# Attention scores on four quarters of the TensorE array (64 queries by 192 keys) in place of two row halves (128 queries by 256 keys)

## The chip, the cores and the metric

The program runs on one core of a Trainium2 chip. The metric is device time in microseconds of one execution; lower is better.

## What is computed

A two-layer decoder trunk over 1024 tokens of width 1024, in fp32. Layer 0 mixes retention and RWKV-7 heads, layer 1 is sliding-window attention with a learned sink per head; each layer ends with a SwiGLU feed-forward block. The change is in the attention:

```python
# SWA_WINDOW = W = 128, 16 query heads, 4 key/value heads, head size 64
kb, vb = with_prev(k), with_prev(v)          # own block of 128 keys and the one before
s = jnp.einsum('bnqhgd,bnkhd->bnhgqk', q, kb).astype(jnp.float32) * HEAD_DIM ** -0.5
rel = qi + W - kj
band = (rel >= 0) & (rel < W)
valid = band[None] & ((jnp.arange(NB)[:, None, None] > 0) | (kj[None] >= W))
s = jnp.where(valid[None, :, None, None], s, -jnp.inf)
m = jnp.maximum(jnp.max(s, axis=-1, keepdims=True), sink)
e = jnp.exp(s - m)
p = e / (jnp.sum(e, axis=-1, keepdims=True) + jnp.exp(sink - m))
o = jnp.einsum('bnhgqk,bnkhd->bnqhgd', p.astype(vb.dtype), vb)
```

So each query sees exactly 128 keys: query t of a block sees its own block's keys 0..t and the earlier block's keys t+1..127.

## The kernel before, in words

Activations lie with features on partitions and tokens along the free dimension. The projections and feed-forward products are done as three fp32r matmuls per 128x512 tile (high and low parts, lines 1298, 1300, 1301 and 445 to 448); attention's own matmuls are plain fp32, and the trace shows each of those as two MATMUL records, each with a weight load. TensorE (PE) runs nearly all the time.

Attention (`attn`, line 1679) is called for the two halves of 512 tokens, hf = 0 and hf = 1. Each call works through 16 blocks, one per key/value head g and 128-query block b (g outer). A block holds 4 query heads; they lie in pairs i on the two partition halves e, and the keys of a head are kept on both halves (tiles kc and ks). Block j goes through three stages, shifted against each other, in a generator loop (line 1761): `turn(j-2)`, `out(j-3)`, `scores(j)`.

- `scores(j)` (line 1693): for each i and each e one matmul of 128 queries against 256 keys (contraction 64, so the two e are on the two row halves of the array) into the PSUM tile of e, tags "r" and "c", one buffer each (lines 1702 to 1709). Then the band is folded to 128 columns: ACT copies the earlier block's half to s (line 1715), and DVE overwrites with the own block's half where the key is not later than the query (COPY_PREDICATED, line 1716). The first 128 tokens (hf = 0, b = 0: blocks 0, 4, 8 and 12, called first blocks below, `k0 = 1`) have no earlier block: there the matmuls take 128 keys, and DVE adds a mask of 0 and -1e30 (line 1713), without ACT. Then row maximum (1719), sink (1721, 1722), four exponentials on ACT (1725), sum and reciprocal (1726, 1727), and the scaling of s, half on POOL and half on DVE (1729).
- `turn(j)` (line 1734): four PE transposes of s (1739), and DVE multiplies the result by the two triangle masks (1741).
- `out(j)` (line 1743): probabilities times values on the two column halves of the array (1751), evacuated by ACT (1757) and DVE (1758).

The fill between the stages are projections and feed-forward tiles of the same layer. The order of PE's instructions in this part is written out by hand, the table ATTN_ORDER (line 135): `39,40:4` takes 4 matmuls in turn from PSUM tiles number 39 and 40 (`queue`, line 326). The orders of DVE, ACT and POOL come from the scheduler of the language.

```python
blocks = [(g, b) for g in range(4) for b in range(4)]
...
for j in range(n + 3):
    if 0 <= j - 2 < n:
        turn(j - 2)
    if 0 <= j - 3 < n:
        n8 = n8 or outs()
        out(j - 3)
    if j < n:
        scores(j)
```

Of the kernel before, what the change touches and what calls it, by code (L numbers as in the profile page):

```python
# [52 lines left out]
def make_consts():  # L53
    c = np.zeros((P, NCO), np.float32)

    def put(name, v):
        o, w = CO[name]
        c[: v.shape[0], o : o + w] = v.reshape(v.shape[0], w)
# [36 lines left out]
        g2[64:, p] = gm[2 * p + 1]  # L95
    put("gam", g2)
    own = np.tri(P, dtype=np.float32)
    put("amask", np.concatenate([own, np.where(own > 0, 0.0, -1e30), own.T, 1.0 - own.T], axis=1))
    put("eps", np.tile(np.array([[RMS_EPS, RET_EPS, RWKV_EPS, math.log(0.5)]], np.float32), (P, 1)))
    return c  # L100

# [31 lines left out]


ATTN_ORDER = """
# [13 lines left out]
"""  # L149


# [102 lines left out]
class Kern:  # L254
# [32 lines left out]
    def mm(self, out, lhsT, rhs, **kw):  # L287

        i = self.nc.tensor.matmul(out, lhsT, rhs, **kw)  # L289
        self.order(out, i)  # L290
        n = 1
        for v in rhs.shape[1:]:
            n *= v
        if rhs.dtype == F32R:
            self.plan.now += 0.000443 * n
        else:
            self.plan.now += max(0.05, 0.00167 * n * (0.6 if lhsT.shape[0] <= 64 or lhsT.shape[1] <= 64 else 1.0))
# [1312 lines left out]
    def attn_open(self, ap):  # L1610
        nc = self.nc
        m = self.const(ap, "amask").rearrange("p (m o t) -> p m o t", m=4, o=1)
        self.own, self.add = (m[:, i].to_broadcast([P, 2, P]) for i in range(2))
        self.sides = [m[:, i].to_broadcast([P, 4, P]) for i in (3, 2)]
        self.sink = self.t(ap, [P, 16], "sink")
        nc.scalar.dma_start(self.sink, self.A["sinks"].to_broadcast([P, 16]))
        self.nsink = self.t(ap, [P, 16], "nsink")
        nc.vector.tensor_scalar(out=self.nsink, in0=self.sink, scalar1=-1.0, scalar2=None, op0=ALU.mult)
        self.b8 = self.t(ap, [P, 8], "b8")
        nc.vector.tensor_scalar(  # L1620
            out=self.b8, in0=self.pv[:, PV["bqkv"] : PV["bqkv"] + 8], scalar1=0.125, scalar2=None, op0=ALU.mult
        )
        self.pk = self.pvt = None
        self.akv, self.aq, self.ch = {}, ([], []), {}
# [54 lines left out]
    def attn(self, hf, ap, outs, fill):  # L1679
# [13 lines left out]
        def scores(j):  # L1693
# [2 lines left out]
            g, b = blocks[j]  # L1696
            ti, rg = g // 2, g % 2
            k0 = first(b)
            kw = slice(P * k0, 256)
            s = sm[j] = self.t(ap, [P, 4, P], "s", 3)  # L1700
            pss = [self.pst("rc"[e], [P, 2, 256]) for e in range(2)]
            for i in range(2):
                for e in (1, 0):
                    a = slice(64 * e, 64 * e + 64)
                    src = (kc if e == rg else ks)[ti]
                    mm(
                        pss[e][:, i, kw], qt[2 * g + i][a, P * b : P * b + P], src[a, P * b + P * k0 : P * b + 256],
                        start=True, stop=True,
                    )
            for e in range(2):  # L1710
                o = s.rearrange("p (i e) k -> p e i k", e=2)[:, e]
                if k0:
                    V.tensor_tensor(out=o, in0=pss[e][:, :, P:], in1=self.add, op=ALU.add)
                else:
                    S.copy(o, pss[e][:, :, :P])
                    V.copy_predicated(o, self.own.bitcast(mybir.dt.uint32), pss[e][:, :, P:])
            st4 = self.t(ap, [P, 4, 4], "st4", 4)
            m, den, es = st4[:, 0, :], st4[:, 1, :], st4[:, 2, :]
            V.tensor_reduce(out=m, in_=s, axis=AX.X, op=ALU.max, negate=True)
# [325 lines left out]
```

## Time and profile before

| | |
|---|---|
| median of 3 runs | 2278.35 us (2278.09 to 2280.45) |
| the profiled execution's own time | 2278.55 us |
| its span | 2276.8 us |
| PE busy | 2247.2 us, 99% of the span |
| DVE, ACT, POOL busy | 1677.0, 1023.6, 999.3 us |
| granted TensorE clock | 0.998 of full speed over the span |
| attention's part of the span | about 1362 to 1646 us |

The span is what the trace covers; the execution's own time is 1.75 us longer. A matmul's end is modelled in this trace and overlaps its successor, so how long PE takes for a group is read from the start of one instruction to the start of the next.

### The profile page before, as it was taken

The numbers are of one execution on the slowest core, as the hardware profiler recorded it, in microseconds if no ns is written. First come the engines' busy times: TensorE is split into PE (matmuls) and PEld (weight loads), VectorE is DVE, ScalarE is ACT, GpSimd is POOL, SyncE is SP. The second block draws the span as 40 slices with busy tenths as digits, with TensorE's granted clock in tenths as the row PEclk, the third lists the DMA queues.
The fourth block names the chain that finished last, engine by engine and source line by source line (L and its number), as shares of the span: only waits on it lengthen the run. The fifth ranks groups of instructions, "written<-read, shape, count | busy, mean of one in ns | idle before, by whom it ended". The sixth has DMA issues, their size and how long they took to land.

```text
span 2276.8 us, 35457 instructions
## 1 busy us (share of the span) xinstructions
PE 2247.2 (99%) x12944; PEld 1796.9 (79%) x12944; DVE 1677.0 (74%) x2600; ACT 1023.6 (45%) x1943; POOL 999.3 (44%) x796
## 2 busy tenths in 40 slices
PE   8999999999999999999999999999999999999998
PEld 6777777778878888888888887687788888888886
DVE  7877965876667358888885967857657788888866
ACT  5454544434455333333343466547654333333335
POOL 3123221212341067777777600103103677777675
PEclk9999999999999999999999999999999999999999
DMA  8565644444356455655767342123246466557663
GB/s 282 187 215 196 206 157 135 141 125 128 134 185 217 168 179 206 215 208 208 261 221 260 113 125 72 53 93 126 100 141 226 172 214 215 209 199 287 228 220 116
DMA packets 170333, 406.53 MB, mean 179 GB/s; under 512 B 43184, under 2 KB 45744, under 8 KB 170160
## 3 DMA queue, kind: packets, MB, share of 16 engines
q1 hardware_dynamic: 166752, 397.59, 50.7%
q10 hardware_dynamic: 2832, 4.59, 0.6%
q8 instruction: 103, 1.69, 0.3%
q0 software_dynamic: 576, 2.10, 0.2%
q14 instruction: 70, 0.57, 0.1%
HBM read 275.61 MB, written 123.21 MB: 175 GB/s over the span
## 4 chain that ended last, share of the span: by engine, by line
PE 80%; DVE 8%; ACT 3%; DMA 3%; issue 3%; POOL 1%; SPq 1%; DVEq 0%; POOLq 0%; ACTq 0%
PE ps_f L289 10%; PE ps_m L1298 7%; PE ps_m L1301 7%; PE ps_m L1300 7%; PE ps_f L1298 6%; PE ps_m L289 6%; PE ps_f L1300 6%; PE ps_f L1301 6%; PE ps_f L448 2%; PE ps_f L445 2%; PE ps_f L447 2%; PE ps_r L1301 2%; PE ps_r L1298 2%; PE ps_c L1301 2%; PE ps_r L1300 2%
## 5 line engine op out<-in xcount | busy, mean ns | idle before, releaser
L289 PE MATMUL ps_f<-n,w 128*128 128x512 f32 x1440 | 359.7, 404 | 8.5 <-ACT w L430 5.8
L289 PEld LDWEIGHTS ps_f<-n,w 128*128 128x128 f32 x1440 | 268.4, 190 | 82.5 <-issue 12.6
L431 POOL TENSOR_TENSOR w<-wr,w 128x512 fp32r<-128x512 f32 x63 | 86.7, 1383 | 301.1 <-ACT w L430 299.3
L430 ACT CAST w<-wr 128x512 fp32r<-128x512 f32 x231 | 141.2, 618 | 165.6 <-PE ps_f L448 58.6
L431 DVE TENSOR_TENSOR w<-wr,w 128x512 fp32r<-128x512 f32 x168 | 120.7, 721 | 61.3 <-ACT w L430 60.7
L1298 PE MATMUL ps_f<-n,w 128*128 128x512 f32 x415 | 164.4, 396 | 0.0
L1300 PE MATMUL ps_f<-n,w 128*128 128x512 f32 x415 | 162.8, 392 | 0.0
L1301 PE MATMUL ps_f<-n,w 128*128 128x512 f32 x415 | 162.6, 392 | 0.0
L431 POOL TENSOR_TENSOR w<-wq,w 128x512 fp32r<-128x512 f32 x91 | 130.4, 1444 | 32.7 <-ACT w L430 32.7
L1298 PE MATMUL ps_m<-n,w 128*128 128x512 f32 x333 | 130.6, 392 | 0.2 <-DMA n<-hc 0.2
L1300 PE MATMUL ps_m<-n,w 128*128 128x512 f32 x333 | 129.6, 389 | 0.0
L1301 PE MATMUL ps_m<-n,w 128*128 128x512 f32 x333 | 129.6, 390 | 0.0
L1308 DVE TENSOR_TENSOR nq<-ps_m,u 128x512 f32<-128x512 f32 x88 | 58.9, 684 | 93.6 <-PE ps_m L1301 93.5
L1729 POOL TENSOR_TENSOR s<-s,st 128x256 f32<-128x256 f32 x32 | 22.9, 715 | 186.4 <-DVE st L1727 76.5
L462 POOL TENSOR_TENSOR n<-nq,n 128x512 fp32r<-128x512 f32 x60 | 100.0, 1678 | 7.7 <-ACT n L460 7.6
L1493 POOL TENSOR_TENSOR w<-wd,w 128x512 fp32r<-128x512 f32 (+1 forms) x62 | 86.7, 1408 | 33.9 <-ACT w L1492 31.6
L1298 PEld LDWEIGHTS ps_f<-n,w 128*128 128x128 f32 x415 | 77.9, 188 | 20.8 <-issue 3.4
L1298 PE MATMUL ps_m<-cb,w 128*128 128x512 f32 x236 | 91.9, 389 | 0.3 <-DVE nq L1308 0.3
L1300 PEld LDWEIGHTS ps_f<-n,w 128*128 128x128 f32 x415 | 77.9, 188 | 18.0 <-issue 2.3
L1301 PE MATMUL ps_m<-cb,w 128*128 128x512 f32 x236 | 91.8, 389 | 0.0
L1300 PE MATMUL ps_m<-cb,w 128*128 128x512 f32 x236 | 91.8, 389 | 0.0
L1301 PEld LDWEIGHTS ps_f<-n,w 128*128 128x128 f32 x415 | 77.9, 188 | 16.8 <-issue 0.7
(523 smaller groups left out, 6421.2 us busy)
## 6 DMA issues: line engine op xcount, KB each, us to landing
hc<-n SPq DMA_DIRECT2D x84, 512.0 KB, 3.4
wsp<-w SPq DMA_DIRECT2D x54, 512.0 KB, 3.5
w<-wsp SPq DMA_DIRECT2D x54, 512.0 KB, 3.4
n<-hc SPq DMA_DIRECT2D x54, 512.0 KB, 6.4
wq<-in_w_gate SPq DMA_DIRECT2D x44, 512.0 KB, 4.5
u<-u SPq DMA_DIRECT2D x88, 256.0 KB, 3.0
ha<-hc SPq DMA_DIRECT2D x34, 512.0 KB, 5.3
hid<-n SPq DMA_DIRECT2D x66, 256.0 KB, 2.0
```

Of the source, the lines that this page charges most:

```text
L289: i = self.nc.tensor.matmul(out, lhsT, rhs, **kw)
L430: nc.scalar.copy(hi[:, :n], raw[:, c])
L431: self.lo.tensor_tensor(out=lo[:, :n], in0=raw[:, c], in1=hi.bitcast(F32)[:, :n], op=ALU.subtract)
L445: x = nc.tensor.matmul(ps, hi, rh, start=k == 0, stop=False)
L447: y = nc.tensor.matmul(ps, hi, rl, start=False, stop=False)
L448: z = nc.tensor.matmul(ps, lo, rh, start=False, stop=k == n - 1)
L462: e.tensor_tensor(out=lo, in0=src, in1=hi.bitcast(F32), op=ALU.subtract)
L1298: i = mm(ps, hi, xh, start=first and k == 0, stop=False, skip_group_check=True)
L1300: mm(ps, hi, xl, start=False, stop=False, skip_group_check=True)
L1301: mm(ps, lo, xh, start=False, stop=last and k == len(w) - 1, skip_group_check=True)
L1308: self.last_add = V.tensor_tensor(out=o, in0=x, in1=y, op=ALU.add)
L1493: nc.gpsimd.tensor_tensor(out=lo, in0=v, in1=hi.bitcast(F32), op=ALU.subtract)
```

## The change

The scores of a block are formed by 64 queries (x = 0 and x = 1, the two column halves of the array) in place of 128. Query half 0 needs 192 keys, the earlier block and the first half of its own; query half 1 needs the second half of the earlier block and all of its own. Both are laid into 192 PSUM columns: the columns 0 to 127 hold what is never masked on the diagonal, the columns 128 to 191 the 64 keys on the diagonal. Query half 0 is one matmul of 192 keys, query half 1 one of 128 keys, whose output goes to two runs of 64 columns (0 and 128), and one of 64 keys. The predicated copy now takes the diagonal 64 columns against a mask that is nonzero only in the two diagonal squares. First blocks take four parts (128 and 64, 128 and 64), and get the predicated copies as well as the mask addition.

```diff
+    x = np.arange(P) // 64
+    diag = np.where(x[:, None] == x[None, :], own, 0.0)
+    put("amask", np.concatenate([diag, np.where(x[:, None] > x[None, :], 0.0, -1e30), own.T, 1.0 - own.T], axis=1))
...
 ATTN_ORDER = """
-22:24 27:1 23:4 24:2 26,25:4 27:18 28:4 29:4 30,31:4 27:5 36:16 32:4 33:4 35:1 34:2 35:1 37:4 38:4 39,40:4 36:8 41:24
+20,21:12 22:24 27:1 23:4 24:2 25,26:12 27:18 28:4 29:4 30,31:16 27:5 36:16 32:4 33:4 34,35:12 37:4 38:4 39,40:12 36:8
...
+        self.diag = m[:, 0].rearrange("p o (x t) -> p o x t", x=2).to_broadcast([P, 2, 2, 64])
+        self.add = m[:, 1].to_broadcast([P, 2, P])
...
-            pss = [self.pst("rc"[e], [P, 2, 256]) for e in range(2)]
+            pss = [self.pst("rc"[e], [P, 2, 192]) for e in range(2)]
+            k1 = P * b + P
+            kp = k1 - P * (1 - k0)
             for i in range(2):
-                for e in (1, 0):
-                    a = slice(64 * e, 64 * e + 64)
-                    src = (kc if e == rg else ks)[ti]
-                    mm(
-                        pss[e][:, i, kw], qt[2 * g + i][a, P * b : P * b + P], src[a, P * b + P * k0 : P * b + 256],
-                        start=True, stop=True,
-                    )
+                parts = [(0, slice(kp, kp + 192), slice(0, 192))]
+                if k0:
+                    parts = [(0, slice(k1, k1 + P), slice(0, P)), (0, slice(k1, k1 + 64), slice(P, 192))]
+                parts.insert(1, (1, slice(k1, k1 + P), None))
+                parts.append((1, slice(kp + 64, kp + P), slice(64, P)))
+                for x, kk, c in parts:
+                    for e in (1, 0):
+                        a = slice(64 * e, 64 * e + 64)
+                        o = pss[e][64 * x : 64 * x + 64, i]
+                        o = o[:, c] if c else o.rearrange("p (y t) -> p y t", t=64)[:, 0:3:2]
+                        r = (kc if e == rg else ks)[ti][a, kk]
+                        mm(
+                            o, qt[2 * g + i][a, P * b + 64 * x : P * b + 64 * x + 64],
+                            r if c else r.rearrange("p (y t) -> p y t", t=64), start=True, stop=True,
+                            skip_group_check=True,
+                        )
             for e in range(2):
                 o = s.rearrange("p (i e) k -> p e i k", e=2)[:, e]
                 if k0:
-                    V.tensor_tensor(out=o, in0=pss[e][:, :, P:], in1=self.add, op=ALU.add)
+                    V.tensor_tensor(out=o, in0=pss[e][:, :, :P], in1=self.add, op=ALU.add)
                 else:
                     S.copy(o, pss[e][:, :, :P])
-                    V.copy_predicated(o, self.own.bitcast(mybir.dt.uint32), pss[e][:, :, P:])
+                V.copy_predicated(
+                    o.rearrange("p i (x t) -> p i x t", x=2), self.diag.bitcast(mybir.dt.uint32),
+                    pss[e][:, :, P:].rearrange("p i (o t) -> p i o t", o=1).to_broadcast([P, 2, 2, 64]),
+                )
```

On PE nothing moves except inside the score groups. Block 3's group before (queries, tile q, against keys, tiles kc and ks; the last number is the free size) and now:

```order
L1751 MATMUL ps_y_12985<-pT_12903,vt_12393 64x256 x2
L1706 MATMUL ps_r_12991<-kc_1902_12394,q_1926_12556 128x256
L1706 MATMUL ps_c_12992<-ks_1907_12430,q_1926_12556 128x256
L1706 MATMUL ps_r_12991<-kc_1902_12394,q_1926_12556 128x256
L1706 MATMUL ps_c_12992<-ks_1907_12430,q_1926_12556 128x256
```

```order
L1768 MATMUL ps_y_13015<-pT_12925,vt_12393 64x256 x2
L1719 MATMUL ps_c_13022<-ks_1907_12430,q_1926_12556 64x192
L1719 MATMUL ps_r_13021<-kc_1902_12394,q_1926_12556 64x192
L1719 MATMUL ps_c_13022<-ks_1907_12430,q_1926_12556 64x2x64
L1719 MATMUL ps_r_13021<-kc_1902_12394,q_1926_12556 64x2x64
L1719 MATMUL ps_c_13022<-ks_1907_12430,q_1926_12556 64x64
L1719 MATMUL ps_r_13021<-kc_1902_12394,q_1926_12556 64x64
L1719 MATMUL ps_c_13022<-ks_1907_12430,q_1926_12556 64x192
L1719 MATMUL ps_r_13021<-kc_1902_12394,q_1926_12556 64x192
```

Four matmuls became twelve (the last four are not shown), sixteen in a first block.

On DVE two instructions are added to each first block, between the mask addition and the row maximum. Block 4 before (s is the block's score tile, st its statistics) and now:

```order
L1758 TENSOR_TENSOR n_1999_12981<-ps_y_13045,n_1995_12977 128x2x128
L1713 TENSOR_TENSOR s_13052<-ps_c_13054,c_amask_12331 128x2x128
L1713 TENSOR_TENSOR s_13052<-ps_r_13053,c_amask_12331 128x2x128
L1634 TENSOR_TENSOR kc_2009_13015<-ps_f_13024,rs_12721 128x512
L1719 TENSOR_REDUCE st_2020_13061<-s_13052 128x4
```

```order
L1775 TENSOR_TENSOR n_1999_13011<-ps_y_13083,n_1995_13007 128x2x128
L1727 TENSOR_TENSOR s_13090<-ps_c_13092,c_amask_12331 128x2x128
L1727 TENSOR_TENSOR s_13090<-ps_r_13091,c_amask_12331 128x2x128
L1730 COPY_PREDICATED s_13090<-c_amask_12331,ps_c_13092 128x2x128
L1730 COPY_PREDICATED s_13090<-c_amask_12331,ps_r_13091 128x2x128
L1636 TENSOR_TENSOR kc_2009_13053<-ps_f_13062,rs_12721 128x512
L1736 TENSOR_REDUCE st_2020_13113<-s_13090 128x4
```

The scheduler also sets other DVE and ACT instructions of attention in another order. In block 10 the two triangle multiplications (pT) come ahead of the sum of the exponentials (st from st, then the reciprocal) instead of behind it. Before and now:

```order
L1721 TENSOR_TENSOR st_2086_13454<-st_2086_13454,nsink_12335 128x4
L1634 TENSOR_TENSOR q_2075_13407<-ps_f_13416,rs_12721 128x512
L1722 TENSOR_TENSOR st_2086_13454<-sink_12333,st_2086_13454 128x4
L431 TENSOR_TENSOR w_13707<-wr_13702,w_13707 128x512
L1726 TENSOR_TENSOR st_2086_13454<-st_2086_13454 128x4
L1741 TENSOR_TENSOR pT_13481<-ps_m_13482,c_amask_12331 128x512 x2
L1727 RECIPROCAL st_2086_13454<-st_2086_13454 128x4
```

```order
L1636 TENSOR_TENSOR q_2075_13505<-ps_f_13514,rs_12721 128x512
L432 TENSOR_TENSOR w_13851<-wr_13846,w_13851 128x512
L1738 TENSOR_TENSOR st_2086_13560<-st_2086_13560,nsink_12335 128x4
L1739 TENSOR_TENSOR st_2086_13560<-sink_12333,st_2086_13560 128x4
L1758 TENSOR_TENSOR pT_13587<-ps_m_13588,c_amask_12331 128x512 x2
L1743 TENSOR_TENSOR st_2086_13560<-st_2086_13560 128x4
L432 TENSOR_TENSOR w_13944<-wr_13942,w_13944 128x512
L1744 RECIPROCAL st_2086_13560<-st_2086_13560 128x4
```

POOL's and SP's orders are as before. (Lines 1717 to 1760 of before stand 17 lines further down in the changed kernel.)

## Rows read from the trace of the kernel before

**Rows 1.** The page's head and its first part, busy us per engine.

```profile
span 2276.8 us, 35457 instructions
...
PE 2247.2 (99%) x12944; PEld 1796.9 (79%) x12944; DVE 1677.0 (74%) x2600; ACT 1023.6 (45%) x1943; POOL 999.3 (44%) x796
```

**Rows 2.** Windows: stretch, length, busy us of PE, PEld, DVE, ACT, POOL, clock, DMA.

```profile
1362.00:1382.00 20.00, 20.00 (x98) 15.47 (x98) 12.04 (x26) 13.85 (x34) 1.51 (x2) 1.00 0.24 80
1382.00:1456.00 74.00, 71.64 (x410) 52.12 (x406) 57.89 (x144) 42.88 (x153) 8.16 (x11) 1.00 0.19 62
1456.00:1646.00 190.00, 189.32 (x968) 140.45 (x969) 127.93 (x281) 116.10 (x327) 39.94 (x39) 1.00 0.29 99
```

**Rows 3.** Chain that ended last, 1382 to 1456 us, shares by line.

```profile
by line: ACT s L1725 23.5%; DVE pT L1741 9.3%; DVE st L1719 7.1%; issue 6.4%; DVE w L431 5.6%; DVE s L1716 4.7%; DVE wx L431 4.6%; DVE s L1729 3.9%; DVE n L1758 3.7%; POOL s L1729 3.4%; PE ps_y L1751 2.8%; DVE s L1713 2.7%; DVE st L1726 2.3
```

**Rows 4.** The same chain, 1456 to 1646 us, shares by line.

```profile
by line: PE ps_f L1298 14.0%; PE ps_f L1300 13.5%; PE ps_f L1301 13.2%; PE ps_y L1751 10.7%; PE ps_f L445 9.0%; PE ps_f L448 8.8%; PE ps_f L447 8.7%; PE ps_r L1706 7.4%; PE ps_m L1739 5.3%; PE ps_c L1706 2.5%; ACT s L1725 1.5%; ACT L1725 0.
```

**Rows 5.** Chain, piece by piece: start us, us, what; block 4.

```profile
1398.23 0.66 DVE s L1713 x2
...
1399.49 0.59 DVE st L1719
...
1404.27 0.89 POOL s L1729
...
1405.20 0.78 PE ps_m L1739 x4
```

**Rows 6.** Who waited for whom on PE, 1355 to 1640 us: total, times, longest.

```profile
PE ps_m L1739 <- POOL s L1729: 2.4, 3, 1.3
PE ps_y L1751 <- DVE n L1758: 0.6, 1, 0.6
```

**Rows 7.** Timeline of PE, scores of block 11: start us, us, what.

```profile
1442.41 0.48 PE L1706 MATMUL ps_r<-kc,q 64*128 64x256 f32 x1
...
1442.73 0.38 PE L1706 MATMUL ps_r<-kc,q 64*128 64x256 f32 x1
...
1442.94 0.38 PE L1706 MATMUL ps_r<-kc,q 64*128 64x256 f32 x1
...
1443.16 0.38 PE L1706 MATMUL ps_r<-kc,q 64*128 64x256 f32 x1
...
1443.47 0.50 PE L1298 MATMUL ps_f<-n,wx 128*128 128x512 f32 x1
```

**Rows 8.** Timeline of PE, scores of block 12, a first block.

```profile
1447.90 0.37 PE L1706 MATMUL ps_c<-kc,q 64*128 64x128 f32 x1
...
1448.54 0.50 PE L1298 MATMUL ps_f<-n,wx 128*128 128x512 f32 x1
```

**Rows 9.** Groups of weight loads, 1355 to 1646 us, shapes apart: busy us, mean ns.

```profile
L1751 PEld LDWEIGHTS ps_y<-pT,vt 128*64 128x64 f32 x232 | 14.2, 136 | 11.3 <-issue 3.9 <-PE ps_m L1739 1.3 <-DVE n L1758 1.1
L1706 PEld LDWEIGHTS ps_c<-kc,q 64*128 64x128 f32 x64 | 10.4, 186 | 1.4 <-issue 0.9 <-DVE pT L1741 0.4
```

**Rows 10.** Timeline of PE in layer 0, retention and RWKV matmuls on array quarters.

```profile
112.71 0.76 PE L289 MATMUL ps_m<-r,Sc 64*64 64x128 f32 x10
113.21 0.27 PE L289 MATMUL ps_m<-UV,GG 64*64 64x64 f32 x2
113.31 0.28 PE L289 MATMUL ps_m<-r,Sc 64*64 64x128 f32 x2
113.32 0.28 PE L289 MATMUL ps_m<-UV,GG 64*64 64x64 f32 x4
113.42 0.28 PE L289 MATMUL ps_m<-r,Sc 64*64 64x128 f32 x2
113.43 0.28 PE L289 MATMUL ps_m<-UV,GG 64*64 64x64 f32 x4
```

**Rows 11.** Timeline of DVE, two predicated copies of one block.

```profile
1432.41 0.44 DVE L1716 COPY_PREDICATED s<-c_amask,ps_c 128x256 f32<-128x256 uint32 x1
1432.74 0.44 DVE L1716 COPY_PREDICATED s<-c_amask,ps_r 128x256 f32<-128x256 uint32 x1
```

More of the change, by code (lines that the diff above doesn't have):

```diff
@@ L97, in make_consts @@
     own = np.tri(P, dtype=np.float32)
-    put("amask", np.concatenate([own, np.where(own > 0, 0.0, -1e30), own.T, 1.0 - own.T], axis=1))
+    x = np.arange(P) // 64
+    diag = np.where(x[:, None] == x[None, :], own, 0.0)
+    put("amask", np.concatenate([diag, np.where(x[:, None] > x[None, :], 0.0, -1e30), own.T, 1.0 - own.T], axis=1))
     put("eps", np.tile(np.array([[RMS_EPS, RET_EPS, RWKV_EPS, math.log(0.5)]], np.float32), (P, 1)))
@@ L1612, in attn_open @@
         m = self.const(ap, "amask").rearrange("p (m o t) -> p m o t", m=4, o=1)
-        self.own, self.add = (m[:, i].to_broadcast([P, 2, P]) for i in range(2))
+        self.diag = m[:, 0].rearrange("p o (x t) -> p o x t", x=2).to_broadcast([P, 2, 2, 64])
+        self.add = m[:, 1].to_broadcast([P, 2, P])
         self.sides = [m[:, i].to_broadcast([P, 4, P]) for i in (3, 2)]
@@ L1698, in scores @@
             k0 = first(b)
-            kw = slice(P * k0, 256)
             s = sm[j] = self.t(ap, [P, 4, P], "s", 3)
-            pss = [self.pst("rc"[e], [P, 2, 256]) for e in range(2)]
+            pss = [self.pst("rc"[e], [P, 2, 192]) for e in range(2)]
+            k1 = P * b + P
+            kp = k1 - P * (1 - k0)
             for i in range(2):
-                for e in (1, 0):
-                    a = slice(64 * e, 64 * e + 64)
-                    src = (kc if e == rg else ks)[ti]
-                    mm(
-                        pss[e][:, i, kw], qt[2 * g + i][a, P * b : P * b + P], src[a, P * b + P * k0 : P * b + 256],
-                        start=True, stop=True,
-                    )
+                parts = [(0, slice(kp, kp + 192), slice(0, 192))]
[14 more added lines that the diff above has]
+                        )
             for e in range(2):
```

23 rows, old and new, of the table ATTN_ORDER are left out of this document.

## The prediction

> **What bounds the kernel now.** I read the busy times first: PE is at work for 99% of the span [rows 1], so at first sight every microsecond taken from PE comes off the total. The windows over attention's part show where that fails: between 1382 and 1456 us PE is idle for 74.00 - 71.64 = 2.4 us, between 1456 and 1646 us for 0.7 us, before 1382 us not at all, always at the full clock [rows 2]. The list of waits says what it waits for: three times a transpose stands until POOL has scaled s, 2.4 us in all [rows 6]. Then the chain of waits, stretch by stretch. From 1382 to 1456 us it runs through ACT's exponentials and DVE's mask, maximum and triangle work; the score matmuls (line 1706) are not among its larger entries [rows 3]. From 1456 to 1646 us it is PE almost alone, score matmuls included [rows 4]. So attention has two regimes. In the middle stretch the softmax of one block after another sets the pace and PE has some slack; in the long one behind it PE sets the pace. The three waits belong to the blocks 4, 8 and 12, the first blocks: for block 4 the chain goes from the mask addition (1398.23) through maximum and exponentials to POOL (1404.27) and then to the waiting transpose (1405.20) [rows 5].
>
> **The score groups on PE.** A block of 256 keys takes PE from 1442.41 to 1443.47, the start of the next product: 1.06 us [rows 7]. Each of the four matmuls shows as two passes, and the two row halves run side by side, so four passes follow one another; their starts lie 0.215 us apart once the first weights are in (1442.73, 1442.94, 1443.16), that is 0.86 us of streaming, and the other 0.20 us goes to the first weight load, which nothing covers, and to the change to and from the other array shape. In a first block of 128 keys the group takes 1448.54 - 1447.90 = 0.64 us [rows 8].
>
> After the change a row half holds two column halves. If all four quarters stream at once, the time is that of the longer quarter. The pace of a pass on a quarter is in the trace: passes of 128 columns start 0.11 us apart and those of 64 columns 0.055 to 0.06 us [rows 10]. Query half 1 needs per pair i two passes of 128 and two of 64 columns: 2 x 0.11 + 2 x 0.058 = 0.335 us; query half 0 two passes of 192, 2 x 0.16 = 0.32 us (0.215 x 192/256 = 0.16). Two pairs: 0.67 us. The load of 64 columns of weights is recorded as 136 ns against 186 for 128 [rows 9], so the uncovered first load shrinks by 0.05 us and 0.15 us stay at the ends. A group then takes 0.67 + 0.15 = 0.82 us: 0.24 us less in an ordinary block, 0.18 us more in a first block, where 192 columns replace 128. With 28 ordinary and 4 first blocks that is 6.7 - 0.7 = 6.0 us of PE time, the most the change can give.
>
> That all four quarters do run at once is the term on which this rests. Attention itself uses only row halves or column halves. But at 113 us in layer 0, matmuls whose row half and column half are equal (line 1222, r and Sc) overlap with matmuls whose halves are opposite (line 936, UV and GG): between 113.31 and 113.42 two passes of the first kind and four of the second start, each kind at its own pace of 0.11 and 0.055 us [rows 10]. I take the full overlap.
>
> The order matters too: the instructions of the second query half stand behind both passes of the first in the program. In the same rows UV and GG stand behind all of r and Sc in program order, and their first passes (113.21) start before the last ones of r and Sc (113.31, 113.42) [rows 10]. So a quarter that is free does not wait for an older instruction of another quarter. The Trainium skill's page TensorE: Matmul & The Clock Gate, Part 3, says otherwise: matmuls start in program order, "strict FIFO, no reordering". By that rule the sum would lose the whole gain (first rival); the trace disagrees with it here, and I follow the trace.
>
> **The predicated copies.** Their count per ordinary block is unchanged, and so are their 256 elements. A first block gets two more, between mask addition and maximum. Their starts lie 0.33 us apart [rows 11], so two cost 0.66 us of DVE. In the blocks 4, 8 and 12 they stand in the very chain that ends in the wait of PE [rows 5, 6]; block 0 has no such wait. Lower bound 0, if the other order of DVE's instructions makes room elsewhere; upper bound 3 x 0.66 = 2.0 us. I take 2.0, because the maximum cannot start before them. The four ACT copies stay, ahead of the predicated copies as before.
>
> **Where it lies.** Up to 1382 us (blocks 0 and 1): 0.18 - 0.24 = -0.1 us. From 1382 to 1456 us (blocks 2 to 13, three of them first blocks) PE saves 9 x 0.24 - 3 x 0.18 = 1.6 us, but I cost this at nothing: each of PE's savings there ends in a longer wait for POOL, and the chain through DVE grows by 2.0 us. Late next is the transpose of a first block, with a longer wait than now. From 1456 us on (blocks 14 to 31) 18 x 0.24 = -4.3 us come through. What follows in the feed-forward part starts from PE, so the gain stays. The sum: -0.1 + 2.0 - 4.3 = **-2.4 us**.
>
> The scheduler's other order on DVE and ACT moves single instructions of 0.3 to 0.7 us across the chain, both ways: in block 10 the triangle products go ahead of the sum of the exponentials, into the time in which DVE waits for ACT, a gain; elsewhere an evacuation comes ahead of a reciprocal, a loss. I cost it at zero with 1 us either way, about two instructions of that size [rows 5]. In the last stretch one wait of 0.6 us for the evacuation of ps_y stands already [rows 6]; savings just ahead of it can be lost there, 2 x 0.24 = 0.5 us.
>
> The sum stands against the profiled execution's own time of 2278.55 us: 2276.15. That execution is 0.2 us above the median, so for the median I say **2276.0 us**.
>
> **The rivals.** (1) *More cover than I think.* If DVE's reordering hides the extra copies, 2.0 us fall away: 2274.0; if the softmax chain gets shorter still, so that PE's 1.6 us in the middle count too, all 6.0 us come through: 2272.4. For it: DVE is idle for 16 us of the 74 in the middle stretch [rows 2]. Against it: that idle time is DVE waiting for the exponentials of the block whose maximum it just formed. Chance 0.25.
>
> (2) *Passes start in program order.* Then the second query half can begin only with the second pass of the first, at 0.16 us; its four passes start at 0.16, 0.27, 0.38 and 0.44, and the next pair cannot start before 0.44. A group takes 2 x 0.44 + 0.06 + 0.15 = 1.09 us, 0.03 more than now, and 0.45 more in a first block. The sum is +0.5 (18 x 0.03) +0.5 (blocks 0 and 1) +2.0: 2281.3, a small loss. The change would then not do what it says. Rows 10 speak against it. Chance 0.08.
>
> (3) *The column halves take turns*, because two streams per row half are one too many for these keys and this PSUM tile: both query halves write one tile, whereas the overlapping kinds in [rows 10] write two. Then a group takes 2 x (0.32 + 0.335) + 0.15 = 1.46 us, 0.40 more (0.82 more in a first block): +7.2 behind 1456 us, +1.2 before 1382 us, and in the middle 9 x 0.40 + 3 x 0.82 - 2.4 of idle time = +3.7, together 2290.5. It decides as soon as a group takes over 1.2 us: 18 x 0.14 + 2.0 = 4.5. Against it: the output products on column halves (line 1751) stream two different operands into one tile side by side already. Chance 0.06.
>
> (4) *The split output is slow.* The matmul of 128 keys writes two runs of 64 PSUM columns, a form that no row shows. At half pace its passes would take 0.22 us, the longer quarter 1.11 us and the group 1.26, 0.20 more than now (0.62 more in a first block): +3.6, +0.8 and +2.0 in the three stretches, 2284.8. The page PSUM — Partial Sum Buffer of the Trainium skill, Specifications, warns that a non-contiguous pattern "slows matmuls significantly"; no run here shows it, and each run here is 64 words long. Chance 0.04.
>
> **How the numbers follow.** My forecast has 0.57. About 0.2% (4.6 us) is what a measurement of this kernel can tell from no change: faster means below 2273.8, slower above 2282.9. Of rival 1 I put 0.17 below that line and 0.08 above it. Rivals 3 and 4 are slower, 0.10. The rest, 0.57 + 0.08 + 0.08 = 0.73, is within. The range reaches from 2272.4 (all PE time) to 2278.5 (forecast, plus 1 us of reordering, 0.5 us lost before ps_y and 1 us, four lost savings of 0.24, at other waits behind 1456 us); rivals 2 to 4 stay out.
>
> **What would show it.** The score groups about 0.82 us from first start to the next product, in all blocks alike; passes of the second query half starting before the second passes of the first. The waits of line 1739's transposes for POOL up from 2.4 us to 6 us or so, still three. The stretch that now runs from 1382 to 1456 us some 2 us longer, and what follows it up to the last block 4.3 us shorter. Wrong if the groups take over 1 us (rivals 2 to 4), if the waits for POOL do not grow (rival 1), or if a new wait shows behind 1456 us.

## The result, and the profile after

| | before | after |
|---|---|---|
| median of the runs | 2279.56 us (9 runs, 2278.09 to 2280.75) | 2285.09 us (9 runs, 2283.27 to 2288.93) |
| ratio, with its 95% interval | | 1.0026 [1.0016, 1.0037] |
| profiled execution, its span | 2278.55 us, 2276.8 us | 2285.57 us, 2283.5 us |

The change made the kernel 0.26% slower, some 6 us. The forecast was 2276.0 us with a range up to 2278.5 us, so it missed both the size and the sign.

The page's head and first part of the changed kernel, to be read beside [rows 1]:

```profile
span 2283.5 us, 36588 instructions
...
PE 2245.1 (98%) x13488; PEld 1800.8 (79%) x13488; DVE 1685.5 (74%) x2608; ACT 1022.5 (45%) x1943; POOL 1000.1 (44%) x796
```

PE's busy time is 2.1 us less than before and yet the span is 6.7 us longer. So PE waits more. The windows (columns as in [rows 2]; the stretches are those of before, at the places to which the same work has moved) tell where:

```profile
1362.00:1382.00 20.00, 20.00 (x136) 15.75 (x134) 12.02 (x27) 13.52 (x34) 1.50 (x2) 1.00 0.25 81
1382.00:1459.00 77.00, 72.06 (x628) 54.65 (x626) 61.69 (x151) 43.04 (x154) 7.15 (x11) 0.98 0.19 60
1459.00:1653.00 194.00, 187.71 (x1256) 142.66 (x1256) 128.12 (x280) 115.26 (x326) 40.55 (x40) 1.00 0.30 98
```

The middle stretch is 3 us longer, with 77.00 - 72.06 = 4.9 us of idle PE in place of 2.4, and its mean clock is 0.98, which was 1.00. The stretch behind it was to become 4.3 us shorter; it is 4 us longer, with 6.3 us of idle PE in place of 0.7. (At 1459 us the third wait for POOL has 0.7 us still to go; cut at its end, 1459.68 us here and 1456.04 us before, what follows up to the last output pass grows from 196.2 to 199.8 us.) The waits of PE from 1355 to 1650 us (columns as in [rows 6]) name four kinds where there were two:

```profile
PE ps_m L1756 <- POOL s L1746: 5.6, 3, 2.1
PE ps_r L1719 <- DVE s L1730: 2.1, 5, 0.5
PE ps_f L1299 <- ACT u L1465: 2.0, 1, 2.0
PE ps_y L1768 <- DVE n L1775: 1.5, 3, 0.8
```

The first is the wait of the first blocks, grown as forecast. The second and third are new: the scores (now line 1719) wait five times for a predicated copy on DVE (line 1730), and a product of the feed-forward part waits once for ACT. The chain that ended last says the same of the last stretch. From 1459 to 1653 us its list of shares begins with ACT's exponentials, 8.6%, which had 1.5% in [rows 4], where PE stood almost alone:

```profile
by line: ACT s L1742 8.6%; PE ps_f L446 8.3%; PE ps_f L449 8.3%; PE ps_f L448 8.2%; PE ps_f L1299 8.0%; PE ps_f L1301 8.0%; PE ps_f L1302 7.7%; PE ps_y L1768 5.4%; DVE pT L1758 5.2%; DVE s L1730 4.1%; DVE st L1736 3.1%; PE ps_c L1719 3.0%; 
```

**The score group does what was forecast.** The timeline of PE, scores of block 3 (start us, us, what), beside [rows 7]:

```profile
1389.81 0.37 PE L1719 MATMUL ps_c<-ks,q 64*64 64x192 f32 x1
...
1389.82 0.32 PE L1719 MATMUL ps_c<-ks,q 64*64 64x128 f32 x1
...
1389.98 0.27 PE L1719 MATMUL ps_c<-ks,q 64*64 64x128 f32 x1
...
1390.02 0.32 PE L1719 MATMUL ps_c<-ks,q 64*64 64x192 f32 x1
...
1390.09 0.22 PE L1719 MATMUL ps_c<-ks,q 64*64 64x64 f32 x1
...
1390.64 0.50 PE L1301 MATMUL ps_f<-n,wx 128*128 128x512 f32 x1
```

The group takes 1390.64 - 1389.81 = 0.83 us against 1.06 before, and so do the undisturbed groups of the other blocks, first ones (0.64 before) too. Both query halves start together (1389.81 and 1389.82), and the second pass of query half 1 (1389.98) starts before the second pass of query half 0 (1390.02), which is older in the program. The split output costs nothing: its pass of 128 columns is followed after 0.11 us (1389.98 to 1390.09), the pace of [rows 10].

**The first new wait.** At five places in the last stretch the score groups of two blocks stand close together, 2.4 to 3.3 us from start to start; they are called a pair here. Timeline of DVE and PE at the first pair:

```profile
1578.17 0.45 DVE L1730 COPY_PREDICATED s<-c_amask,ps_c 128x256 f32<-128x256 uint32 x1 [0.48 <-ACT s L1729]
1578.51 1.28 DVE L1758 TENSOR_TENSOR pT<-ps_m,c_amask 128x512 f32<-128x512 f32 x2
...
1579.18 0.54 PE L1719 MATMUL ps_c<-kc,q 64*64 64x192 f32 x2
...
1579.71 0.43 DVE L1730 COPY_PREDICATED s<-c_amask,ps_r 128x256 f32<-128x256 uint32 x1
...
1580.20 0.37 PE L1719 MATMUL ps_r<-ks,q 64*64 64x192 f32 x1 [0.48 <-DVE s L1730]
...
1581.02 0.50 PE L1299 MATMUL ps_f<-n,w 128*128 128x512 f32 x1
```

and DVE before, at the same pair (line 1741 is the triangle products):

```profile
1574.46 0.44 DVE L1716 COPY_PREDICATED s<-c_amask,ps_c 128x256 f32<-128x256 uint32 x1
1574.79 1.28 DVE L1741 TENSOR_TENSOR pT<-ps_m,c_amask 128x512 f32<-128x512 f32 x2
```

The scheduler has put two triangle products (line 1758) between the two predicated copies of the pair's first block; in the kernel before both copies (the second at 1574.46) stand ahead of the products. The scores of the second block need ps_r, which has one buffer, and that buffer is free only when the second copy is done. PE starts the group with two passes into ps_c at 1579.18 and goes on at 1580.20. The list of waits counts only the idle part, 0.48 us here and 2.1 us in all; from its start to the next product the group takes 1581.02 - 1579.18 = 1.84 us in place of 0.83, and the five such groups together are 4.7 us longer.

**The second new wait.** ACT and DVE, 1563 to 1574 us, after:

```profile
1563.16 0.61 ACT L431 CAST wx<-wr 128x512 fp32r<-128x512 f32 x1
1565.23 1.28 ACT L1742 ACT_TABLE_LOAD   x1 [1.45 <-DVE st L1738]
1566.53 0.40 ACT L1742 ACTIVATE s<-s,st 128x128 f32<-128x128 f32 x1
...
1573.79 0.56 ACT L1465 COPY u<-ps_f 128x512 f32<-128x512 f32 x1
```

```profile
1563.20 0.69 DVE L1736 TENSOR_REDUCE st<-s 128x4 f32<-128x512 f32 x1
1563.92 1.23 DVE L1738 TENSOR_TENSOR st<-st,nsink 128x4 f32<-128x4 f32 x1
```

PE, behind that copy of u:

```profile
1574.40 0.50 PE L1299 MATMUL ps_f<-n,w 128*128 128x512 f32 x1 [1.98 <-ACT u L1465]
```

and the same place in ACT's timeline before:

```profile
1560.29 0.61 ACT L430 CAST wx<-wr 128x512 fp32r<-128x512 f32 x1
1560.92 1.28 ACT L1725 ACT_TABLE_LOAD   x1
1562.31 0.40 ACT L1725 ACTIVATE s<-s,st 128x128 f32<-128x128 f32 x1
```

Between sigmoid and exponential ACT loads a table, 1.28 us. Before, the load ran beside DVE's minimum. After, ACT stands idle for 1.45 us until the minimum (line 1738) is done and only then loads. The built programs tell why; ACT's instructions at this place with their waits, first before, then after:

```
L1725 ACTIVATE s_2249_14447,st4_2252_14458<-s_2249_14447,st4_2252_14458 128x128 [waits DVE_49]
```

```
L1742 ACT_TABLE_LOAD [waits DVE_49]
L1742 ACTIVATE s_2249_14631,st4_2252_14650<-s_2249_14631,st4_2252_14650 128x128 [waits Activation_49]
```

The new predicated copy writes s through a pattern of 128x2x2x64, and with it the exponential waits for both, for DVE and for ACT's own copy. (Presumably the framework no longer sees that the predicated copy covers what ACT's copy wrote; the runs show only that the shape brings the wait.) Of the two waits one stands at the exponential and the other at the instruction ahead of it, and where that is a table load, the load waits too. The semaphores in the traces say the same: of the five table loads ahead of exponentials none waits before, and all five wait for DVE after. What it delays is a whole pair: the copy of u that frees a tile for PE's next product stands in ACT's queue behind the exponentials of the second block (1573.79), and these come later by what the first block's came later.

**The third loss.** The clock, in windows of 4 us (columns as in [rows 2], the clock third from the end):

```profile
1402.00:1406.00 4.00, 2.56 (x38) 1.63 (x36) 2.32 (x7) 3.17 (x13) 0.59 (x1) 1.00 0.41 131
1406.00:1410.00 4.00, 3.66 (x28) 2.06 (x32) 2.98 (x7) 0.37 (x1) 0.28 (x1) 0.60 0.00 0
1410.00:1414.00 4.00, 4.00 (x31) 3.31 (x24) 2.25 (x8) 2.89 (x12) 0.61 (x1) 0.97 0.02 4
```

Behind the wait of block 4 (PE idle from 1404.56 to 1406.34) the granted clock fell from 2.4 to 1.2 GHz (it is 0.50 from 1408 to 1410 us). That cost 4 x 0.40 + 4 x 0.03 = 1.7 us of work at full speed.

### The profile page after: what moved, and what is told of

Its sections match the earlier page's. It is cut to its first block, busy times and chain, and to the rows that moved or that the text cites. A ratio compares the mean times of both kernels' runs of the same rounds, so it can differ in the third digit from the quotient of the medians.

```text
span 2283.5 us, 36588 instructions
## 1 busy us (share of the span) xinstructions
PE 2245.1 (98%) x13488; PEld 1800.8 (79%) x13488; DVE 1685.5 (74%) x2608; ACT 1022.5 (45%) x1943; POOL 1000.1 (44%) x796
## 4 chain that ended last, share of the span: by engine, by line
PE 79%; DVE 11%; ACT 4%; DMA 2%; issue 2%; SPq 1%; POOL 1%; DVEq 0%; POOLq 0%; ACTq 0%
PE ps_f L290 9%; PE ps_m L1299 8%; PE ps_m L1302 7%; PE ps_m L1301 7%; PE ps_f L1299 5%; PE ps_f L1301 5%; PE ps_f L1302 5%; PE ps_m L290 5%; PE ps_r L1299 2%; PE ps_f L449 2%; PE ps_f L446 2%; PE ps_r L1302 2%; PE ps_f L448 2%; PE ps_r L1301 2%; PE ps_c L1302 2%; PE ps_c L1299 2%
```

## The experiments

Theory A: the quarters save their 0.24 us a group, and four things take it away: the order of DVE and ACT (the copy behind the triangle products), the second wait of the exponentials (the table load), the two extra copies of the first blocks, and a fall of the clock behind the longer waits. The rivals: one of them is the whole cause; or the quarters themselves cost something elsewhere.

Two measures are used. One is the ratio of all runs to the kernel before on the same chip. Its intervals are some 0.1% either way and the differences 0.01 to 0.26%, so the traces have to carry the argument. The other measure is steadier, the length of attention in the profiled execution, from the start of its first score pass to the end of its last output pass, which lies behind the 1646 us where the rows of before stop: 1362.66 to 1652.25 us before, 289.6 us; 1363.18 to 1659.45 us after, 296.3 us, that is +6.7 us. The rest of the span, the same code in all kernels, took 1985.2 to 1990.9 us in these executions. Where the clock fell in attention (read from windows as above), 1.7 us are taken off for each fall and the figure is called net; the changed kernel is then at 294.6 us. Differences are taken before rounding. Line numbers shift with the edits.

Each kernel has one profiled execution. How far it can be trusted shows when attention is cut at the end of the third wait for POOL. Behind it, the kernel before takes 196.2 us without the extra copies and 196.2 with them, the quarters 193.7 and 193.6: the copies of the first blocks change nothing there, and the figures repeat within 0.1 us. Up to it, the four kernels with quarters and extra copies (rows 2, 4, 5 and 7 of the table) take 96.5, 98.2, 96.2 and 96.6 us with 1, 2, 1 and 1 falls; less 1.7 us a fall that is 94.8, 94.8, 94.5 and 94.9. So a fall there does cost the whole 1.7 us. (In the quarters with the short chain the fall lies behind that wait, where 1.7 us is taken without such a comparison.)

| run | ratio to before [95%] | attention, us | falls | net, us |
|---|---|---|---|---|
| before | | 289.6 | 0 | 289.6 |
| after | 1.0026 [1.0016, 1.0037] | 296.3 | 1 | 294.6 |
| quarters alone | 0.9988 [0.9979, 0.9996] | 287.2 | 0 | 287.2 |
| after, order of before | 1.0017 [1.0008, 1.0026] | 294.2 | 2 | 290.8 |
| after, one wait | 1.0012 [1.0002, 1.0021] | 293.7 | 1 | 292.0 |
| before, two waits | 1.0007 [0.9998, 1.0016] | 291.9 | 0 | 291.9 |
| quarters and extra copies | 0.9999 [0.9990, 1.0008] | 290.2 | 1 | 288.5 |
| quarters, own order | 1.0010 [1.0001, 1.0019] | 292.3 | 1 | 290.6 |
| before, order of after | 1.0024 [1.0015, 1.0033] | 294.7 | 0 | 294.7 |
| before, extra copies | 1.0009 [1.0000, 1.0017] | 293.0 | 1 | 291.3 |
| quarters, short chain | 0.9988 [0.9979, 0.9997] | 287.5 | 1 | 285.8 |
| before, short chain | 0.9997 [0.9988, 1.0006] | 289.0 | 0 | 289.0 |
| quarters, short chain, earlier subtraction | 0.9988 [0.9979, 0.9997] | 286.0 | 0 | 286.0 |
| before, short chain, earlier subtraction | 0.9997 [0.9988, 1.0006] | 288.3 | 0 | 288.3 |

### The quarters alone

The changed kernel, less everything that is not PE's. A list fixes the order of DVE and ACT in this part of the program, instruction by instruction, to that of the kernel before; the predicated copy writes 128x2x128; first blocks get two parts of 128 keys and one mask addition.

```diff
+        K.line(mark, "DVE", DVE_ORDER)
+        K.line(mark, "Activation", ACT_ORDER)
...
-                V.copy_predicated(
-                    o.rearrange("p i (x t) -> p i x t", x=2), self.diag.bitcast(mybir.dt.uint32),
...
+                    V.copy_predicated(
+                        o, self.diag.bitcast(mybir.dt.uint32),
...
-                    parts = [(0, slice(k1, k1 + P), slice(0, P)), (0, slice(k1, k1 + 64), slice(P, 192))]
...
+                parts = [(x, slice(k1, k1 + P), slice(0, P)) for x in range(2)]
...
```

> The quarters alone: DVE and ACT run in the order of the kernel before, the exponentials wait for DVE alone, and the first blocks (0, 4, 8, 12) have one mask add over 128 keys and no predicated copy, so only the passes of TensorE differ from before. Theory A (the quarters do their part, and order, waits and the first blocks took it away): the gain behind the first third comes through, 18 x 0.24 = 4.3 us, so about 2275 us (2273.5 to 2276.5), POOL waits still three and near 2.4 to 4 us. Rival (the quarters cost elsewhere, by the clock or by starts of the groups): not under 2278.5 us.

Measured: 2276.79 us (11 runs) against 2279.41 us (33 runs) of before, ratio 0.9988 [0.9979, 0.9996], attention 287.2 us. Faster by 0.12%, so the quarters cost nothing elsewhere; but the median lies just above A's range, and attention gains 2.4 us and not 4.3. The waits of PE, 1355 to 1655 us:

```profile
PE ps_m L1823 <- POOL s L1813: 4.7, 3, 1.7
PE ps_y L1835 <- DVE n L1842: 1.6, 4, 0.9
PE ps_f L1367 <- ACT u L1533: 0.5, 1, 0.5
PE ps_m L1735 <- ACT nq L1705: 0.3, 1, 0.3
```

The wait for POOL is 2.3 us longer than before: the middle stretch swallows what PE saves there, as forecast. Behind it 0.5 us goes into a wait for ACT's u that was not there, and the wait for ps_y grows by 1.0 us, from 0.6 [rows 6] to 1.6. (The 0.3 us for ACT's nq lies in the middle stretch.)

### The order alone, the wait alone

The changed kernel with the two order lists (the extra copies straight behind their mask additions), and apart from that the changed kernel with the copy's output as 128x2x128 and its own order.

```diff
+        K.line(mark, "DVE", DVE_ORDER)
+        K.line(mark, "Activation", ACT_ORDER)
```

> The changed kernel with the order of the kernel before on DVE and ACT, the extra predicated copies straight behind their mask adds; the second wait of the exponentials stays. Theory A: the five waits of the second score group of a pair on the predicated copy go (in the trace 0.33 to 0.48 us idle each, about 0.7 us each with the restart), 3 to 4 us less than the changed kernel: about 2281.5 us (2280.5 to 2283). Rival B (the order is the whole cause): 2275 to 2276.5 us. Rival C (the order matters nothing): 2284 to 2286 us.

```diff
-                    o.rearrange("p i (x t) -> p i x t", x=2), self.diag.bitcast(mybir.dt.uint32),
+                    o, self.diag.bitcast(mybir.dt.uint32),
```

> The changed kernel with the predicated copy's output as 128x2x128 in place of 128x2x2x64: the exponentials then wait for DVE alone and the table load no longer stands behind a wait; the order on every engine is that of the changed kernel. Theory A: the load of 1.28 us runs beside the minimum again, the 2.0 us wait of the feed-forward group on ACT falls to under 1 us, 1 to 2 us less than the changed kernel: about 2283.7 us. Rivals B and C: no difference (2284.5 to 2285.7 us).

With the order of before: 2283.53 us, between the expectations of A and C, because the clock fell twice in the profiled execution (mean clock over the 11 runs 0.9967, of before 0.9981). Net of that, attention is 294.6 - 290.8 = 3.8 us shorter than the changed kernel's, as A had it, and the wait of ps_r is gone from the list; the wait for ACT is not:

```profile
PE ps_m L1824 <- POOL s L1814: 5.9, 3, 2.3
PE ps_f L1367 <- ACT u L1533: 2.4, 2, 2.0
PE ps_y L1836 <- DVE n L1843: 1.9, 4, 0.8
```

With one wait: 2281.99 us, attention 2.5 us shorter, more than A's 1 to 2. Here it is the other way round, the wait for ACT is at 0.5 us and the wait of ps_r stays:

```profile
PE ps_m L1756 <- POOL s L1746: 4.9, 3, 1.9
PE ps_r L1719 <- DVE s L1730: 2.2, 5, 0.5
PE ps_y L1768 <- DVE n L1775: 0.8, 3, 0.3
PE ps_f L1299 <- ACT u L1465: 0.5, 1, 0.5
```

So these are two causes, apart from each other, and with one wait none of the five table loads waits any more. One line, the shape of an output, is worth 2.5 us.

### The same two on the kernel before

```diff
...
-                    V.copy_predicated(o, self.own.bitcast(mybir.dt.uint32), pss[e][:, :, P:])
+                    V.copy_predicated(
+                        o.rearrange("p i (x t) -> p i x t", x=2),
+                        self.own4.bitcast(mybir.dt.uint32),
+                        pss[e][:, :, P:].rearrange("p i (x t) -> p i x t", x=2),
+                    )
```

> The kernel before with the predicated copy's operands as 128x2x2x64 (same elements): the exponentials of the ordinary blocks get the second wait, on ACT itself, and five table loads stand behind the wait for DVE; the order on every engine stays that of before. Theory A: slower than before by what of 5 x 1.28 us is not covered, 1 to 2 us: 2280.3 to 2281.5 us, with a wait of TensorE on ACT or POOL behind 1550 us that the kernel before lacks. Rival: no difference, 2279 to 2280 us.

Measured: 2282.05 us. The ratio, 1.0007 [0.9998, 1.0016], does not tell this from no change; the trace does. ACT's timeline and PE's new wait:

```profile
1560.42 0.61 ACT L430 CAST wx<-wr 128x512 fp32r<-128x512 f32 x1
1562.49 1.28 ACT L1730 ACT_TABLE_LOAD   x1 [1.46 <-DVE st L1726]
```

```profile
PE ps_f L1298 <- ACT u L1464: 1.5, 1, 1.5
```

Same instructions, same order, same elements written, and the load waits 1.46 us for DVE; all five table loads wait for DVE here. Attention is 291.9 us, +2.4, a little over A's 1 to 2.

```diff
+        K.line(mark, "DVE", DVE_ORDER)
+        K.line(mark, "Activation", ACT_ORDER)
```

(on the kernel before, with the lists taken from the changed kernel)

> The kernel before, all its instructions, in the order of the changed kernel on DVE and ACT. Theory A: the order alone puts the second score group of the pairs behind the predicated copy that stands behind two triangle products, five times some 0.7 us: 2282.5 to 2283.5 us, a stretch near 293 us. Rival (the order only hurts the quarters, whose groups come earlier and in another sequence): 2279 to 2280.5 us.

Measured: 2284.58 us, 1.0024 [1.0015, 1.0033], attention 294.7 us: +5.1, more than A's 3.4. The order alone makes the kernel before as slow as the changed one. The wait is longer here (1.1 us a time, against 0.5) because the group's first pass in PE's queue is one into ps_r, where the changed kernel has two into ps_c ahead of it:

```profile
PE ps_r L1774 <- DVE s L1784: 5.5, 6, 1.1
PE ps_m L1807 <- POOL s L1797: 2.2, 3, 0.9
```

### The extra copies, and all but the order

The quarters alone with the first blocks as in the changed kernel (its extra copies, its 192 columns); the quarters alone without the order lists, in an order near that of the changed kernel but not the same in every place; and the kernel before with a second write of the own scores in its first blocks, held in its order by the lists of before:

```diff
...
                     V.tensor_tensor(out=o, in0=pss[e][:, :, P:], in1=self.add, op=ALU.add)
+                    V.copy_predicated(o, self.own.bitcast(mybir.dt.uint32), pss[e][:, :, P:])
...
```

> The changed kernel with the order of before and the exponentials waiting for DVE alone; the two extra predicated copies of the first blocks stay. Beside the run with the quarters alone it has only these copies more. Theory A: they lengthen the chain of blocks 4 and 8 by about 0.6 us each, block 12 hardly, so the three waits for POOL are together some 1.2 us longer (near 6 us) and the stretch from the first score pass to the last output pass is near 288.4 us, about 2278 us in all; a fall of the granted clock behind one of the waits adds 1.7 us more. Rival (the copies are free, the first blocks are not a cause): as with the quarters alone, 287.2 us and 2276.8 us.

> The quarters with one wait and without the extra copies, but in the order that the scheduler itself gives. Theory A: against the quarters alone it lacks only the order of before, worth 3.8 us between the changed kernel and the run with the order alone: the waits for the predicated copy in the pairs are back, the stretch near 291 us, about 2280.5 us, slower than the kernel before. Rival (order and wait only hurt together): under 2278.5 us.

> The kernel before with two more predicated copies in the first blocks behind their mask adds (they write the same own scores once more), order otherwise as before. Theory A: blocks 4 and 8 each wait 0.6 us longer for POOL, block 12 up to as much: 1.2 to 2.0 us, stretch 290.8 to 291.6 us, about 2281 us; a fall of the clock behind a wait adds 1.7 us. Rival (the copies are free): 289.6 us and no difference.

The copies: 2278.79 us and 288.5 us net, +1.4 over the quarters alone; on the kernel before 2281.68 us and 291.3 us net, +1.8, with one fall of the clock in each. The rival (free copies) falls. Their three waits, of the quarters and of the kernel before:

```profile
PE ps_m L1824 <- POOL s L1814: 5.9, 3, 2.1
```

```profile
PE ps_m L1808 <- POOL s L1798: 4.3, 3, 2.0
```

All but the order: 2281.48 us, 1.0010 [1.0001, 1.0019], slower than before as A said, 290.6 us net, 3.5 us over the quarters alone. The order and the wait add up; the rival that they only hurt together falls.

### A shorter chain in the first blocks

On DVE, blocks 4, 8 and 12: the reciprocal and the scaling move straight behind the sum, from behind the triangle products (in block 8 from behind a weight split and a subtraction), and one weight split of block 4, the subtraction that forms the low part of a weight tile, moves behind the minimum; with the quarters, and on the kernel before. DVE's order in block 8, by the lines of before:

```diff
 L1726 TENSOR_TENSOR st<-st
+L1727 RECIPROCAL st<-st
+L1729 TENSOR_TENSOR s<-s,st
 L431 TENSOR_TENSOR w<-wr,w
 L1758 TENSOR_TENSOR n<-ps_y,n
-L1727 RECIPROCAL st<-st
-L1729 TENSOR_TENSOR s<-s,st
```

> The quarters alone (as in that run), and on DVE the reciprocal and the scaling of the first blocks 4, 8 and 12 moved straight behind the sum, ahead of the triangle products, and in block 4 one weight split behind the minimum. Theory A: the middle stretch gives nothing because this chain ends last there; with 1.9, 1.0 and 1.2 us taken from the three chains the waits of 1.6, 1.72 and 1.42 us shrink to about 0, 0.7 and 0.2 us, and the quarters' 0.24 us a group come through there as well: stretch near 283.5 us, about 2273 us. Rival (the middle waits for something else, such as the exponentials or TensorE itself): stretch 287 us, no difference to the quarters alone.

> The kernel before with the same move of reciprocal and scaling on DVE. Theory A: its three waits of 0.52, 1.32 and 0.56 us go almost, 2.0 to 2.4 us less than before: stretch 287.3 us, about 2277 us; the quarters on top of it (the other run of this pair) are then worth 3.5 to 4 us in place of 2.4. Rival: no difference to before, or the quarters still worth 2.4 us or less.

The waits for POOL shrink as expected, 4.7 to 1.6 us with the quarters and 2.4 to 0.5 us before, but the wait for ps_y grows, to 3.6 and 1.8 us: the subtraction that frees it now stands behind the moved work. Net 285.8 and 289.0 us, medians 2276.01 and 2277.20 us, both short of A's 283.5 and 287.3 us. Of the 3 us taken from POOL's wait 1.3 reach the end, of the 1.9 us before 0.6. So in the last pair the subtraction (line 1758 of before) also moves ahead of the weight split (line 431).

> The quarters with the short chain of blocks 4, 8 and 12, and there the subtraction that frees the output's PSUM tile moved ahead of the weight split on DVE. Theory A: of the two new waits of 1.0 us on that tile 0.6 us each go, stretch 284.6 us where the clock does not fall (286.3 with one fall), 2274.5 to 2275.5 us. Rival (what is saved here comes back in the next wait again): stretch 285.8 us net of the clock, 2276 us.

> The kernel before with the short chain and the same move of the subtraction: its one wait of 1.0 us on the output's tile shrinks to about 0.4 us. Theory A: stretch 288.4 us, about 2277 us, so that the quarters are worth 3.5 to 4 us with both moves made. Rival: no difference to the short chain alone (289.0 us).

286.0 us (no fall) and 288.3 us; 2275.85 and 2278.76 us. With the quarters the move brought nothing net, the rival's case; on the kernel before it took 0.7 us off attention, as A had it, while the ratio stays at 0.9997. The waits that stand now with the quarters:

```profile
PE ps_y L1835 <- DVE n L1842: 2.5, 6, 0.9
PE ps_m L1823 <- POOL s L1813: 1.6, 2, 0.8
```

The quarters are worth 288.3 - 286.0 = 2.3 us here, 2.4 without the moves, and 3.1 with the short chain alone (net of its one fall), not the 3.5 to 4 of the expectation. The version with all of it has the lowest median, 2275.85 us, and is faster than the kernel before (0.9988 [0.9979, 0.9997]), which the changed kernel is not; the quarters alone are so too, and the runs, on different chips, don't tell these two apart.

## Why the prediction was wrong

In order of its own steps:

- **Score groups, 1.06 to 0.82 us: right.** 0.83 us, all four quarters at once; rivals 2, 3 and 4 fall by the same rows. The Trainium skill's page TensorE: Matmul & The Clock Gate, Part 3, has matmuls start in program order, and the trace disagrees here as well (1389.98 before 1390.02); the case is the prediction's rival 2, which it calls the first rival there. The Trainium skill's page PSUM — Partial Sum Buffer, Specifications, says that a non-contiguous pattern slows matmuls significantly, and for runs of 64 columns this did not show (0.11 us per pass).
- **Extra copies, +2.0 us: right in mechanism, somewhat large.** The waits for POOL went from 2.4 to 5.6 us (forecast 6), still three; 2.3 us of that growth came with the quarters alone, and in time the copies cost 1.4 to 1.8 us. What the step left out is the clock: a fall to 1.2 GHz behind one of these waits cost 1.7 us.
- **Middle stretch, PE's 1.6 us worth nothing: right.** In the quarters alone the wait for POOL grew by 2.3 us. But the reason given, one softmax chain, is too narrow: with that chain shortened the next wait, for ps_y, took most of it.
- **"From 1456 us on ... 18 x 0.24 = -4.3 us come through": wrong.** Alone, the quarters gained 2.4 us in all of attention. Where PE arrives earlier it meets ps_y, which has one buffer, and ACT: 1.0 and 0.5 us more of waiting. The sum had nothing for this; the range had 0.5 us for ps_y and 1 us for other waits, which is as much as the waits showed.
- **"The scheduler's other order ... I cost it at zero with 1 us either way": the step that failed most.** It cost 3.8 us, and 5.1 us put on the kernel before; the prediction's own sign of being wrong, a new wait behind 1456 us, came with it. Counting instructions of 0.3 to 0.7 us on the softmax chain looked at the wrong wait: what matters is which single-buffered tile the moved instruction frees, and who needs it next.
- **Not in the sum at all: the second wait of the exponentials,** 2.4 to 2.5 us. The prediction weighed the order of the instructions and not what each of them waits for.

The sum by the measured terms: -2.4 (quarters) + 3.8 (order) + 2.4 (waits) + 1.4 (copies) + 1.7 (clock) = +6.9 us against +6.7 us of attention in the two profiled executions. They also lie where they should: up to the end of the third wait for POOL attention is 3.1 us longer, the copies and the clock (1.4 + 1.7); behind it 3.6 us, the order and the waits less the quarters (3.8 + 2.4 - 2.4 = 3.8).

## What to carry to other kernels

When a scheduler reorders an engine, look for instructions that free a tile with one buffer, and follow who writes that tile next; the length of the moved instruction did not tell it here. Compare the waits of the built program too, not its order alone: a changed access pattern of the same elements can add a wait to a third instruction, and a wait ahead of a table load takes the load out of the time that hid it. And a saving on the engine that seems to be the bound need not come through whole: here 1.5 us of some 4 went into waits for a tile with one buffer and for ACT.

## What the runs showed of the hardware

- **The clock can fall behind short stalls.** In each of the seven profiled executions in which it fell in attention, it fell to 1.2 GHz shortly behind waits of PE in the first blocks (1.71 to 2.27 us long in six of them; in the seventh two waits of 0.86 and 1.0 us close together), and each fall cost 1.7 us of work at full speed. In the other seven, whose longest such wait was 0.52 to 1.72 us, it did not fall there. Not every long wait was followed by a fall (2.11 us in the changed kernel and 2.14 us in the quarters with extra copies were not), so which stall brings one is left open. In the changed kernel with the order of before it fell twice:

```profile
1406.00:1410.00 4.00, 3.68 (x28) 2.08 (x32) 2.85 (x7) 0.37 (x1) 0.27 (x1) 0.59 0.00 0
...
1436.00:1440.00 4.00, 3.91 (x38) 2.84 (x39) 2.19 (x6) 2.04 (x11) 0.04 (x1) 0.68 0.01 2
```

- **A minimum of four columns took 1.23 us,** where its median is 0.16: it began at 1563.92, while POOL ran a subtraction, and ended with it:

```profile
1563.86 1.28 POOL L432 TENSOR_TENSOR wx<-wr,wx 128x512 fp32r<-128x512 f32 x1 [1.70 <-ACT wx L431]
```

The Trainium skill's page SBUF — State Buffer, SBUF: two separate sides, says that a DVE instruction with two SBUF inputs and a GpSimd instruction that reads SBUF share a port pair, which the one that starts first holds for its whole instruction. The trace agrees (1563.86 + 1.28 = 1565.14 and 1563.92 + 1.23 = 1565.15). It is this stretched minimum for which the table load waited. The kernel before has it at the same place too (1.24 us from 1561.04 on, beside POOL's 1.28 us from 1560.97 on), but there the load ran beside it.
